# A fixed TensorE order for a two-layer hybrid trunk, and the first norm weight applied at the split

## The chip, the cores and the metric

One core of a Trainium2 chip runs the whole program. The metric is the device time of one execution in microseconds, as the median of several runs. The engines are TensorE (PE, with its weight loads as PEld), VectorE (DVE), ScalarE (ACT), GpSimd (POOL) and SyncE (SP); SP issues the DMAs in the kernel before, one after the other, and a DMA whose buffer isn't free yet holds up those behind it.

## The reference

Two layers over 256 tokens of width 1024, in float32. Each layer is a token mixer and a channel mixer, each between two RMS norms:

```python
def rms_norm(x, g):
    y = xf * lax.rsqrt(jnp.mean(xf * xf, axis=-1, keepdims=True) + NORM_EPS)
    return (y * g.astype(jnp.float32)).astype(x.dtype)

for l in range(DEPTH):
    h = rms_norm(x, ln_mix_pre[l])
    x = x + rms_norm(hybrid_mixer(h, ...), ln_mix_post[l])
    h = rms_norm(x, ln_ffn_pre[l])
    x = x + rms_norm(conv_ffn(h, ...), ln_ffn_post[l])
```

`hybrid_mixer` projects h by `w_in` (2726 columns) for three groups of heads: six with a T5 relative bias on their logits (with 256 tokens and blocks of 256 they are plain causal attention), four with low-rank latents of q and kv and a rotary part, six with a decay from a cumulative sum of log-sigmoids. Their outputs are joined and multiplied by `w_o`. `conv_ffn` multiplies by `w_up` (5632 columns), runs a causal convolution of width 3 over tokens, forms gelu(g) * val, and multiplies by `w_down`.

## The kernel before

**Tiles.** The tokens are two tiles of 128 rows, `xt[0]` and `xt[1]`. `prenorm(t, g)` squares a tile on ACT (`rstd2`, two halves of 512 columns), makes the factor r on POOL, multiplies by the norm weight and by r on DVE. `to_feat(t, ...)` transposes the result on PE, eight blocks of 128x128 in two banks of four, and `split` makes a rounded part (`xh`, ACT) and the rest (`xl`, DVE) of it. Every product is then made of three: high by high, high by low, low by high (`mm3`, `mm3s`, lines 203 to 213).

**Weights.** They are read in slabs of 256 to 512 KB in a fixed order (`plan`): for each layer `c` (latents), `v`, `qa`, `uq`, `uk`, `f`, `qc`, `o`, and then by pairs of feed-forward columns `g`, `u` and `d`. A slab lands in one of three staging buffers `st` (line 175), and `load_next` splits it into `wh` on ACT (line 193) and `wl` on DVE (line 194), for eight slabs at a time. `slab(key)` asks for five slabs ahead and for two more DMAs.

**The start of layer 0.** SP loads tile 0, the identity, and the norm weight, which `gain` reads as a broadcast to 128 rows; then slabs, tile 1 and small constants. Three matmuls of zeros (line 122) stand at the start of PE. The projection `c` of a tile is four pieces (`nat_piece`, one per slab, six matmuls each of 416 columns), `v` is four of 384. `bias_start` builds the bias table from `oh` and `rel_bias` with a matmul (line 286), writes it out and reads it back shifted as `hk`; `bias_end` takes it up later. `c_norm` and `c_feat` norm and transpose the latents (line 373), `mla_up` and `mla_feat` build the four latent heads, and `qk_group` makes the q and k features that `qk_end` copies out (line 402).

**Attention.** `step(n, per)` makes the logits of pair n of heads (`pair_qk`), fills with pieces of other products from the list `fill` (`pump` takes pieces until their listed cost is used up), transposes the softmax of pair n-1 (`pair_t`, copy `pS` at line 512) and forms its output (`pair_pv`, `mh` and `ml`). `wo_piece(t, k)` is one slab of the output projection. Only here was the order of PE the program's:

```python
        with tc.manual_schedule(engines={mybir.EngineType.PE}):
            for n in range(5):
                step(n, total / 5)
```

Everywhere else a scheduler orders each engine's instructions from its own cost model and from priorities (`first` raises those of a function). **Feed-forward.** `up_nat` makes the first two pairs in the natural layout, `up_feat` transposes them, `up(i)` makes the others; `conv_glu` follows on ACT and DVE, and `down(i, t)` adds a pair into the two banks `ac[t]`. The last pairs of tile 1 are held back (`late`) so that tile 0 can be normed beside them.

## Time and profile before

| what | value |
|---|---|
| median of 3 runs | 671.79 us (671.17 to 673.45) |
| the profiled execution | 671.39 us |
| its span in the trace | 669.6 us |
| PE busy in the span | 633.5 us, 95% |
| DVE, ACT, POOL busy | 455.6, 387.0, 30.3 us |
| read from memory | 108.37 MB |
| mean granted clock of PE | 0.984 |

The span is the stretch that the trace covers; the execution's own time holds it and 1.8 us around it. A busy PE is one whose matmuls overlap in the pipeline, so its share says where it stood still, not how near it is to its peak.

### The profile page before, as it was taken

To read this page: it belongs to the slowest core of one execution; us is meant where nothing else is said; L and a number is where in the kernel's file an instruction comes from. 1 tells how busy PE (TensorE), PEld (TensorE's weight loads), DVE (VectorE), ACT (ScalarE), POOL (GpSimd) and SP (SyncE) were. 2 spreads that over 40 slices of the span, in tenths; PEclk is the share of its full clock that TensorE was granted. 3 is DMA by queue.
4 is the path that set the end of the run, shared out by engine and by line. 5 is a ranking of instruction groups with operands and counts; after the bars stand their busy time and mean duration, and the time that the engine had idled before them with its cause. 6 is when DMAs were issued, how large, how long until landed. Compare 5 with 4: busy or idle time off the path is not lost.

```text
span 669.6 us, 11313 instructions
## 1 busy us (share of the span) xinstructions
PE 633.5 (95%) x4286; PEld 572.5 (85%) x4286; DVE 455.6 (68%) x904; ACT 387.0 (58%) x729; POOL 30.3 (5%) x68
## 2 busy tenths in 40 slices
PE   6399999998999999999999999999899999999996
PEld 4299888767899999999979988876899999999995
DVE  4446577657686777777787758765768687777773
ACT  5246676664675655555475757566476465555541
POOL 1110000011000000000023000001200000000001
PEclk7699999999999999999999999999999999999999
DMA  7747562225556665554457865223455765565411
GB/s 242 241 132 213 161 198 73 64 94 188 163 185 215 212 201 189 187 179 141 148 146 201 223 182 185 73 64 95 154 170 180 230 211 189 188 189 189 156 66 63
DMA packets 79668, 110.16 MB, mean 165 GB/s; under 512 B 3960, under 2 KB 69758, under 8 KB 79614
## 3 DMA queue, kind: packets, MB, share of 16 engines
q1 hardware_dynamic: 79614, 109.44, 52.1%
q8 instruction: 33, 0.54, 0.4%
q14 instruction: 21, 0.17, 0.1%
HBM read 108.37 MB, written 1.06 MB: 163 GB/s over the span
## 4 chain that ended last, share of the span: by engine, by line
PE 75%; DMA 10%; ACT 6%; DVE 4%; issue 2%; POOL 2%; SPq 0%; POOLq 0%; DVEq 0%; ACTq 0%
PE wk L210 15%; PE wk L211 15%; PE wk L213 15%; PE wk L203 7%; PE wk L205 7%; PE wk L204 7%; DMA st<-in_w_in_dram 5%; DMA st<-in_w_up_dram 3%; ACT wh L193 3%; DVE wl L194 3%; ACT scr L232 2%; PE wk L510 1%; PE wk L484 1%; PE wk L519 1%; PE wk L482 1%
## 5 line engine op out<-in xcount | busy, mean ns | idle before, releaser
L194 DVE TENSOR_TENSOR wl<-st,wh 128x1024 fp32r<-128x1024 f32 (+3 forms) x200 | 235.8, 1185 | 111.2 <-ACT wh L193 110.3
L193 ACT ACTIVATE wh<-st 128x1024 fp32r<-128x1024 f32 (+3 forms) x200 | 205.0, 1028 | 109.4 <-PE wk L211 33.6
L210 PE MATMUL wk<-xh,wh 128*128 128x256 f32 x768 | 195.2, 286 | 0.0
L211 PE MATMUL wk<-xl,wh 128*128 128x256 f32 x768 | 192.8, 283 | 0.0
L210 PEld LDWEIGHTS wk<-xh,wh 128*128 128x128 f32 x768 | 146.9, 191 | 2.2 <-issue 0.9
L211 PEld LDWEIGHTS wk<-xl,wh 128*128 128x128 f32 x768 | 147.0, 191 | 1.1 <-issue 0.3
L213 PE MATMUL wk<-xh,wl 128*128 128x256 f32 x768 | 123.7, 283 | 0.0
L213 PEld LDWEIGHTS wk<-xh,wl 128*128 128x128 f32 x768 | 106.0, 192 | 0.3 <-issue 0.3
L203 PE MATMUL wk<-wh,hp 128*128 128x512 f32 x176 | 68.8, 391 | 0.0
L204 PE MATMUL wk<-wl,hp 128*128 128x512 f32 x176 | 68.7, 390 | 0.0
L205 PE MATMUL wk<-wh,hp 128*128 128x512 f32 x176 | 68.6, 390 | 0.0
L210 PE MATMUL wk<-wh,xh 128*128 128x256 f32 (+3 forms) x224 | 67.8, 321 | 0.5 <-ACT xh L216 0.5
L211 PE MATMUL wk<-wl,xh 128*128 128x256 f32 (+3 forms) x224 | 66.8, 317 | 1.5 <-DVE wl L194 1.4
L730 ACT ACTIVATE t<-wk,cv 128x256 f32<-128x256 f32 x88 | 44.3, 557 | 33.0 <-PE wk L213 30.8
L734 DVE SCALAR_TENSOR_TENSOR t<-wk,cv,t 128x255 f32<-128x255 f32 x88 | 41.6, 477 | 31.3 <-ACT t L730 31.3
L213 PE MATMUL wk<-wh,xl 128*128 128x256 f32 (+3 forms) x224 | 47.6, 316 | 0.0
L210 PEld LDWEIGHTS wk<-wh,xh 128*128 128x128 f32 x224 | 43.6, 195 | 3.0 <-issue 1.5
L211 PEld LDWEIGHTS wk<-wl,xh 128*128 128x128 f32 x224 | 43.7, 195 | 2.5 <-DVE wl L194 2.2
L736 DVE SCALAR_TENSOR_TENSOR t<-wk,cv,t 128x254 f32<-128x254 f32 x88 | 41.7, 478 | 1.3
L205 PEld LDWEIGHTS wk<-wh,hp 128*128 128x128 f32 x176 | 33.0, 188 | 7.1 <-DVE hp L217 0.2
L203 PEld LDWEIGHTS wk<-wh,hp 128*128 128x128 f32 x176 | 33.1, 188 | 6.7 <-ACT hp L216 0.4
L204 PEld LDWEIGHTS wk<-wl,hp 128*128 128x128 f32 x176 | 33.1, 188 | 6.1
(136 smaller groups left out, 694.9 us busy)
## 6 DMA issues: line engine op xcount, KB each, us to landing
st<-in_w_up_dram SPq DMA_DIRECT2D x88, 512.0 KB, 4.2
st<-in_w_down_dram SPq DMA_DIRECT2D x44, 512.0 KB, 4.3
st<-in_w_in_dram SPq DMA_DIRECT2D x24, 512.0 KB, 4.7
st<-in_w_o_dram SPq DMA_DIRECT2D x16, 512.0 KB, 4.3
st<-in_w_in_dram SPq DMA_DIRECT2D x8, 416.0 KB, 3.7
st<-in_w_in_dram SPq DMA_DIRECT2D x8, 390.0 KB, 4.8
st<-in_w_in_dram SPq DMA_DIRECT2D x8, 384.0 KB, 3.4
x<-in_x_dram SPq DMA_DIRECT2D x2, 512.0 KB, 3.4
```

The lines of the kernel that those rows point to most:

```text
L193: nc.scalar.activation(h[:, c], st[:, c], AF.Copy)
L194: nc.vector.tensor_tensor(lo[:, c], st[:, c], h[:, c].bitcast(F32), op=ALU.subtract)
L203: nc.tensor.matmul(o, stat[0], mov[0], start=start, stop=False)
L204: nc.tensor.matmul(o, stat[0], mov[1], start=False, stop=False)
L205: nc.tensor.matmul(o, stat[1], mov[0], start=False, stop=stop)
L210: nc.tensor.matmul(o, stat[0], mov[0], start=start and i == 0, stop=False)
L211: nc.tensor.matmul(o, stat[0], mov[1], start=False, stop=False)
L213: nc.tensor.matmul(o, stat[1], mov[0], start=False, stop=stop and i == n - 1)
L232: nc.scalar.activation(junk[:, HALF[i]], src[i], AF.Square, scale=1.0 / 32, accum_out=ms[:, i:i + 1])
L730: nc.scalar.activation(y[:, g, :], u[:, g, :], AF.Identity, scale=cv[:, 88 + cj:89 + cj], bias=cv[:, 132 + cj:133 + cj])
L734: nc.vector.scalar_tensor_tensor(y[:, g, 1:], u[:, g, :S - 1], cv[:, 44 + cj:45 + cj], y[:, g, 1:], op0=ALU.mult, op1=ALU.add)
L736: nc.vector.scalar_tensor_tensor(y[:, g, 2:], u[:, g, :S - 2], cv[:, cj:cj + 1], y[:, g, 2:], op0=ALU.mult, op1=ALU.add)
```

## The change

The order of PE's instructions is the program's order from the start to the end, no longer only in attention. So the order in the text is written out anew in several places:

- Layer 0's norm weight isn't broadcast: `g8` holds it as 8x128, one small transpose makes `gT` (128x8), and `to_feat` applies it per block of 128 in the split (`scale=` on ACT, a scalar operand on DVE). `prenorm` with `g=None` only scales by r.
- Tile 0 is loaded in two halves; the identity, `g8`, `oh` and `rel_bias` come over ACT's queue, the bias table goes over POOL's. The constants `cst` come in two parts, and the loads of norm weights stay at their place in SP's order.
- The first pieces `c` go: tile 0's first three, tile 1's transposes, then both tiles' alternately; `v` alternates by slab; then the bias matmul and both tiles' latents. `after` (new) ties the first slab conversions and tile 1's norm behind given instructions.
- The third `qa` group is filler of step 0, the third `qc` group filler of step 5, and the pieces of `wo` move to steps 6 and 7 and to the unrolled end.
- The feed-forward part starts in another order, `down` runs bank by bank over a pair, and the last late pieces run bank by bank.
- There is one more warm matmul.

The diff, without unchanged lines:

```diff
-from contextlib import ExitStack
+from contextlib import ExitStack, contextmanager
...
     def gain(ap):
...
-        nc.sync.dma_start(g, bcast(ap, D))
+        tc.keep_in_program_order(nc.sync.dma_start(g, bcast(ap, D)))
...
-    nc.sync.dma_start(xt[0], x_v[0])
-    nc.sync.dma_start(ident, cst_d[:, 0:128])
-    g_pre = gain(ln_mix_pre[0])
+    ctx.enter_context(tc.manual_schedule(engines={mybir.EngineType.PE}))
+    g8 = work.tile([8, 128], F32, name="g8", tag="pS", bufs=3)
+    oh = work.tile([32, 256 + HA], F32, name="oh", tag="pr", bufs=5)
+    gT = const.tile([128, 8], F32, name="gT")
+    for c in (slice(0, 512), slice(512, 1024)):
+        nc.sync.dma_start(xt[0][:, c], x_v[0][:, c])
+    nc.scalar.dma_start(ident, cst_d[:, 0:128])
+    nc.scalar.dma_start(g8, ln_mix_pre[0].rearrange("(c p) -> c p", p=128))
+    nc.scalar.dma_start(oh[:, :256], oh_d)
+    nc.scalar.dma_start(oh[:, 256:], rel_bias)
+    g_pre = None
...
-    for i in range(3):
+    for i in range(4):
...
     def scr():
...
+    scaled = [None]
...
     def prenorm(t, g):
...
+        src = xt[t] if g is None else hn
+        if g is not None:
+            for c in HALF:
+                nc.vector.tensor_tensor(hn[:, c], xt[t][:, c], g[:, c], op=ALU.mult)
...
-            nc.vector.tensor_tensor(hn[:, c], xt[t][:, c], g[:, c], op=ALU.mult)
-        for c in HALF:
-            nc.vector.tensor_scalar(hn[:, c], hn[:, c], r, None, op0=ALU.mult)
+            scaled[0] = nc.vector.tensor_scalar(hn[:, c], src[:, c], r, None, op0=ALU.mult)
...
+    ends = []
+    @contextmanager
+    def after(*insts):
+        with ExitStack() as st:
+            for i in insts:
+                st.enter_context(tc.issue_after(getattr(i, "ins", i)))
+            yield
...
-    def to_feat(t, hn, xh, xl):
+    def to_feat(t, hn, xh, xl, g=None):
...
-            s = (slice(None), slice(4 * q, 4 * q + 4), tok(t))
-            split(ps, xh[s], xl[s])
+            if g is None:
+                s = (slice(None), slice(4 * q, 4 * q + 4), tok(t))
+                split(ps, xh[s], xl[s])
+                continue
+            for c in range(4):
+                k = 4 * q + c
+                h, gk = xh[:, k, tok(t)], g[:, k:k + 1]
+                a = nc.scalar.activation(h, ps[:, c, :], AF.Copy, scale=gk)
+                v = nc.vector.scalar_tensor_tensor(xl[:, k, tok(t)], ps[:, c, :], gk, h.bitcast(F32),
+                                                   op0=ALU.mult, op1=ALU.subtract)
+            ends.append((a, v))
...
     def postnorm(t, a, g, dst=None):
...
     def bias_start():
-        oh = t2([32, 256 + HA])
-        nc.sync.dma_start(oh[:, :256], oh_d)
-        nc.sync.dma_start(oh[:, 256:], rel_bias)
...
-        rr = t2([HA, 384])
+        rr = work.tile([HA, 384], F32, name="rr", tag="pr", bufs=5)
...
-        nc.sync.dma_start(sd, rr)
+        nc.gpsimd.dma_start(sd, rr)
...
-        nc.sync.dma_start(hk[0], bass.AP(tensor=sd.tensor, offset=sd.offset, ap=[[1, 128], [384, HA], [1, S]]))
+        nc.gpsimd.dma_start(hk[0], bass.AP(tensor=sd.tensor, offset=sd.offset, ap=[[1, 128], [384, HA], [1, S]]))
...
     def bias_end():
...
+        def small_loads():
+            nc.sync.dma_start(lc[:, :256], bcast(q_norm[l], 256))
+            nc.sync.dma_start(lc[:, 256:384], bcast(kv_norm[l], 128))
+            nc.sync.dma_start(lc[:, 384:390], bcast(b_f[l], 6))
         if l == 0:
...
-            hn = [prenorm(0, g_pre), None]
+            hn = [prenorm(0, None), None]
+            dma_next()
+            nc.sync.dma_start(xt[1], x_v[1])
...
-            nc.sync.dma_start(xt[1], x_v[1])
-            to_feat(0, hn[0], xh, xl)
-            slab((l, "c", 0))
-            hn[1] = prenorm(1, g_pre)
+            small_loads()
+            nc.sync.dma_start(cst[:, C_R:], cst_d[:, 128 + C_R:])
+            ps8 = wk()
+            nc.tensor.transpose(ps8[:, :8], g8, ident[:8, :8])
+            nc.vector.tensor_copy(gT, ps8[:, :8])
+            to_feat(0, hn[0], xh, xl, gT)
+            with after(scaled[0]):
+                load_next()
+            for i in range(2):
+                with after(*ends[i]):
+                    load_next()
+            with after(*ends[1]):
+                hn[1] = prenorm(1, None)
         else:
...
             act_set(EXP_SET)
...
-        nc.sync.dma_start(lc[:, :256], bcast(q_norm[l], 256))
-        nc.sync.dma_start(lc[:, 256:384], bcast(kv_norm[l], 128))
-        nc.sync.dma_start(lc[:, 384:390], bcast(b_f[l], 6))
+        cps = [wk(), wk()]
+        vps = [wk(), wk()]
+        def c_piece(t, h):
+            nat_piece(cps[t], "c", t, 416, h)
+        def v_piece(t, h):
+            nat_piece(vps[t], "v", t, 384, h)
+        def v_end(t):
+            nc.scalar.activation(vs[0][:, 384 * t:384 * t + 384], vps[t][:, :384], AF.Copy)
+        if l == 0:
+            c_piece(0, 0)
+            c_piece(0, 1)
+            c_piece(0, 2)
+            to_feat(1, hn[1], xh, xl, gT)
+            for t, h in ((1, 0), (1, 1), (0, 3), (1, 2), (1, 3)):
+                c_piece(t, h)
+            nc.vector.tensor_copy(identr, ident[:6, :6])
+            cn0 = c_norm(0, cps[0])
+            cn1 = c_norm(1, cps[1])
+            for h in range(4):
+                for t in range(2):
+                    v_piece(t, h)
+            v_end(0)
+            v_end(1)
+            nc.sync.dma_start(cst[:, :C_R], cst_d[:, 128:128 + C_R])
+            bias_start()
+            c_feat(0, cn0)
+            c_feat(1, cn1)
+        else:
+            small_loads()
+            for h in range(4):
+                c_piece(0, h)
+            cn0 = c_norm(0, cps[0])
+            for h in range(4):
+                v_piece(0, h)
+            v_end(0)
+            to_feat(1, hn[1], xh, xl)
+            for h in range(4):
+                c_piece(1, h)
+            cn1 = c_norm(1, cps[1])
+            c_feat(0, cn0)
+            for h in range(4):
+                v_piece(1, h)
+            v_end(1)
+            c_feat(1, cn1)
...
-        cps = nat("c", 0, 416)
-        if l == 0:
-            nc.sync.dma_start(cst, cst_d[:, 128:])
-            nc.vector.tensor_copy(identr, ident[:6, :6])
-            bias_start()
-        cn0 = c_norm(0, cps)
-        vps = wk()
-        for h in range(3):
-            nat_piece(vps, "v", 0, 384, h)
-        to_feat(1, hn[1], xh, xl)
-        nat_piece(vps, "v", 0, 384, 3)
-        nc.scalar.activation(vs[0][:, :384], vps[:, :384], AF.Copy)
-        cps = nat("c", 1, 416)
-        cn1 = c_norm(1, cps)
-        c_feat(0, cn0)
-        vps = nat("v", 1, 384)
-        nc.scalar.activation(vs[0][:, 384:768], vps[:, :384], AF.Copy)
-        c_feat(1, cn1)
...
         if l == 0:
...
-        qk_group("qa", 2, 0)
...
-        def qc_fill(i):
+        def q_fill(nm, i, base):
...
             def piece(a, k0):
...
-                proj(st["ps"][:, a, :], "qc", i, a, k0, xh, xl)
+                proj(st["ps"][:, a, :], nm, i, a, k0, xh, xl)
...
-                    qk_end(i, st["ps"], 6)
-            return [(1.3, lambda a=a, k0=k0: piece(a, k0)) for a in range(2) for k0 in (0, 4)]
-        fill += f_fill(0) + f_fill(1) + qc_fill(0) + [(1.2, fox_sum)] + qc_fill(1)
-        q2 = qc_fill(2)
+                    qk_end(i, st["ps"], base)
+            return [(1.44, lambda a=a, k0=k0: piece(a, k0)) for a in range(2) for k0 in (0, 4)]
+        fill += q_fill("qa", 2, 0) + f_fill(0) + f_fill(1) + q_fill("qc", 0, 6) + [(1.0, fox_sum)]
+        q2 = q_fill("qc", 1, 6)
...
-            fill += [(0.4, lambda i=i: fox_bias(i)), q2[i]]
+            fill += [q2[i], (0.5, lambda i=i: fox_bias(i))]
...
-        with tc.manual_schedule(engines={mybir.EngineType.PE}):
-            for n in range(5):
-                step(n, total / 5)
+        for n in range(5):
+            step(n, total / 5)
+        pump(1e9)
+        fill += q_fill("qc", 2, 6)
+        step(5, 5.7)
+        pump(1e9)
+        for n, wo in ((6, ((0, 0), (0, 1), (0, 2), (0, 3))), (7, ((0, 4), (0, 5)))):
+            fill += [(1.4, lambda t=t, k=k: wo_piece(t, k)) for t, k in wo]
+            step(n, 1.4 * len(wo))
...
-            for n, wo in ((5, ((0, 0), (0, 1), (0, 2))), (6, ((0, 3), (0, 4))), (7, ((0, 5), (1, 0))),
-                          (8, ((0, 6), (1, 1)))):
-                fill += [(1.4, lambda t=t, k=k: wo_piece(t, k)) for t, k in wo]
-                step(n, 1.4 * len(wo))
-                pump(1e9)
-            wo_piece(0, 7)
+        wo_piece(1, 0)
+        pS[7] = pair_t(pr[7])
+        wo_piece(0, 6)
+        ot = wk()[:, :256]
+        pair_pv(hd[7], pS[7], ot)
+        first(split)(ot, mh[:, 7, :], ml[:, 7, :])
+        wo_piece(1, 1)
+        wo_piece(0, 7)
...
-        def down(i, t):
-            for a in range(2):
-                j = 2 * i + a
-                wh, wl = slab((l, "d", j))
-                for n in range(2):
-                    c = slice(n * 512, n * 512 + 512)
+        def down(i, t, ns=(0, 1)):
+            for n in ns:
+                c = slice(n * 512, n * 512 + 512)
+                for a in range(2):
+                    j = 2 * i + a
+                    wh, wl = slab((l, "d", j))
...
+        up_nat(0, 1)
+        up_nat(1, 1)
...
-        up_nat(0, 1)
-        up_feat(0, [wk().rearrange("p (a b) -> p a b", a=2) for _ in range(2)])
-        up_nat(1, 1)
-        us1 = acc()
-        up_feat(1, [us1[a].rearrange("p (a b) -> p a b", a=2) for a in range(2)])
-        ac.extend(acc() for _ in range(2))
+        def feat_us():
+            return [wk().rearrange("p (a b) -> p a b", a=2) for _ in range(2)]
+        up_feat(0, feat_us())
...
+            if i == 2:
+                up_feat(1, feat_us())
+                ac.extend(acc() for _ in range(2))
...
-        for j in late:
-            down(j, 1)
+        down(late.pop(0), 1)
+        for n in range(2):
+            for j in late:
+                down(j, 1, (n,))
```

## Rows read from the trace of the kernel before

**Rows 1.** The page, parts 1 and 5 (mean ns of one, idle before).

```profile
PE 633.5 (95%) x4286; PEld 572.5 (85%) x4286; DVE 455.6 (68%) x904; ACT 387.0 (58%) x729; POOL 30.3 (5%) x68
...
L194 DVE TENSOR_TENSOR wl<-st,wh 128x1024 fp32r<-128x1024 f32 (+3 forms) x200 | 235.8, 1185 | 111.2 <-ACT wh L193 110.3
```

**Rows 2.** Windows of 10 us: engines, PEclk, DMA share, GB/s.

```profile
20.00:30.00 10.00, 0.00 (x0) 0.00 (x0) 4.36 (x11) 3.26 (x7) 1.89 (x4) 0.66 0.96 312
...
180.00:190.00 10.00, 8.43 (x72) 8.23 (x71) 8.20 (x16) 6.83 (x13) 0.00 (x0) 1.00 0.48 159
```

**Rows 3.** Waits of PE over the span: total us, times, longest.

```profile
PE wk L286 <- DMA t<-in_rel_bias_dram: 10.4, 1, 10.4
PE wk L262 <- DVE scr L254: 8.6, 7, 3.9
PE wk L708 <- ACT un L702: 1.6, 1, 1.6
...
PE wk L211 <- DVE wl L194: 1.4, 2, 0.7
PE wk L482 <- ACT q L402: 1.3, 1, 1.3
PE wk L203 <- ACT xh L216: 0.9, 2, 0.5
PE wk L205 <- DVE xl L217: 0.9, 2, 0.5
PE wk L519 <- ACT pS L512: 0.9, 2, 0.5
PE wk L203 <- ACT cT L216: 0.9, 1, 0.9
```

**Rows 4.** Timeline of the first 30 us: start, duration, engine, line.

```profile
1.51 5.09 PE L122 MATMUL wk<-t 128*128 128x512 f32 x6 [1.51 <-DVE t L119]
...
5.88 0.56 POOL L235 TENSOR_TENSOR r<-r,mhalf 128x1 f32<-128x1 f32 x1
8.73 1.29 DVE L252 TENSOR_TENSOR scr<-x,gain 128x512 f32<-128x512 f32 x2 [4.26 <-DMA gain<-in_ln_mix_pre_dram]
...
10.47 1.97 PE L262 MATMUL wk<-ident,scr 128*128 128x128 f32 x8 [3.87 <-DVE scr L254]
...
12.48 0.60 ACT L216 ACTIVATE xh<-wk 128x512 fp32r<-128x512 f32 x1 [0.21 <-PE wk L262]
...
15.69 0.88 DVE L254 TENSOR_SCALAR scr<-scr,r 128x512 f32<-128x512 f32 x2 [0.45 <-POOL r L235]
...
27.15 0.28 ACT L363 ACTIVATE t<-wk 128x128 f32<-128x128 f32 x1 [1.86 <-DVE t L365]
...
28.45 0.35 DVE L365 SCALAR_TENSOR_TENSOR t<-wk,r,lc 128x128 f32<-128x128 f32 x1 [1.33 <-POOL r L222]
```

**Rows 5.** Timeline of PE, 31 to 49 us.

```profile
31.26 0.69 PE L210 MATMUL wk<-wh,xh 128*128 128x384 f32 x1
...
36.90 0.34 PE L210 MATMUL wk<-wh,xh 128*128 128x384 f32 x1
...
38.99 0.35 PE L210 MATMUL wk<-wh,xh 128*128 128x416 f32 x1
...
43.14 0.54 PE L213 MATMUL wk<-wh,xl 128*128 128x416 f32 x2
...
48.02 0.49 PE L373 MATMUL wk<-ident,t 128*128 128x128 f32 x3
```

**Rows 6.** Timeline of PE at the boundary of the layers.

```profile
346.06 1.09 PE L262 MATMUL wk<-ident,scr 128*128 128x128 f32 x8 [0.86 <-DVE scr L254]
...
355.52 1.09 PE L262 MATMUL wk<-ident,scr 128*128 128x128 f32 x8 [0.65 <-DVE scr L254]
```

**Rows 7.** DMA issues: count, KB each, median us to landing.

```profile
st<-in_w_in_dram SPq DMA_DIRECT2D x8, 416.0 KB, 3.7
...
hk<-sd SPq DMA_DIRECT2D x1, 768.0 KB, 4.9
```


## The prediction

> **What bounds the kernel now.** I read the page first. TensorE (PE) is busy 633.5 of 669.6 us [rows 1], so about 36 us of the span hold no matmul, and only those, and stretches at the low clock, can be won: the diff removes no matrix work (it adds one warm matmul and one small transpose). Next I read busy time by stretches of 10 us: between 20 and 30 us PE does nothing at all while the DMA engines are 96% busy [rows 2]. Then the waits of PE, longest in total first [rows 3]. Two thirds of the idle time is at the very start: 10.4 us for the load of `rel_bias`, and within the 8.6 us for `scr` one wait of 3.9 us. The rest are a few waits of some 0.5 to 1.6 us at the seams between stages. No line of that view belongs to the long feed-forward loops.
>
> The timeline of the first 30 us says why [rows 4]. The first tile's factor r is ready at 5.88+0.56 = 6.44 us, but VectorE (DVE) multiplies by the norm weight first, and that 512 KB broadcast lands only at 8.73. The transposes start at 10.47, after the three warm matmuls have run out at 1.51+5.09 = 6.60. Tile 1 is scaled at 15.69. What PE does after that is an order of the scheduler's: the bias-table matmul of line 286 stands ahead of the next weights, and its operand is loaded late on SP's queue. PE resumes with real work at 31.26; a 384-column matmul takes 0.69 us there and 0.34 at 36.90 [rows 5]: for 5.6 us the work ran at the low one of the two clock levels, 1.2 instead of 2.4 GHz, and cost about 2.8 us more. From 48.02, the transposes of the second tile's latents, both kernels do the same matrix work. So I cost the change as the time at which the new kernel gets there, and then the seams.
>
> **The start, step by step.**
> 1. Warm matmuls: six halves took 5.09 us [rows 4], 0.85 each. Eight end at 1.51+6.8 = 8.3 at the low clock.
> 2. Weight taken out of `prenorm`: no wait for the broadcast and no multiplication. The scaled tile is ready at 6.44+0.88 = 7.3 (scaling both halves takes 0.88, as for tile 1 in [rows 4]), so PE, not the tile, decides: transposes begin at 8.3 instead of 10.47, and take 1.97 us at the low clock [rows 4] or 1.1 at the high one [rows 6]. By then PE has worked since 1.51 without a break, and the slow stretch of [rows 5] was over 5.6 us after the work began: I take 1.1 and keep 1.97 for the bound.
> 3. Weight put into the split: eight pieces of 128x128 on ScalarE (ACT), then DVE, instead of two of 128x512. The nearest rows are 0.28 on ACT and 0.35 on DVE [rows 4], so 2.2 and 2.8 us against 2x0.60 on ACT: about 1.0 us more on ACT per tile. The first product needs only two pieces, so it starts near 8.9+0.28x2+0.35 = 9.8.
> 4. Until tile 1 is scaled, the old kernel needed 15.69-10.47 = 5.2 us from the first transposes. The new one needs 1.0 more for the pieces, and zero to two slab conversions come ahead of the squares on ACT (the DVE half of one takes 1.19 at 1024 columns [rows 1], some 1.0 at 832). That puts the scaling at 14.5 to 16.3. If the slabs come later, the third piece of tile 0, which stands ahead of tile 1's transposes, waits for its slab instead. I take 16 for the transposes.
> 5. Transposes 1.1 and the first pieces 0.6 to 0.9: 17.8. Left are 5 of the 8 pieces `c`, 30 matmuls. 24 of them take 38.99 to 43.52, 0.19 each [rows 5]: 5.7 us. The 48 of `v` are 384 columns instead of 416: 0.175 each, 8.4 us. Then the bias matmuls (0.5) and the first tile's latents (0.25): 32.6.
>
> So the common point moves from 48.0 to about 32.5: **15.5 us**. The bounds: if step 4 hid altogether, only the work would be left (transposes 2.2, 48x0.19, 48x0.175, 0.75) and the point would be at 8.3+20.5 = 28.8, 19.2 us earlier. If the clock fell in the wait of step 4, the next 5.6 us would cost 2.8 more, and if the first transposes were slow too and a slab late by one conversion, 2 to 3 us more: 10 us earlier.
>
> Whether the clock holds through such waits of one to three microseconds is open. A wait of 1.6 us at line 708 stood in a stretch with granted clock 1.00 [rows 2, 3], the wait of 10.4 stood before one at 1.2 GHz. The Trainium skill, "TensorE: Matmul & The Clock Gate", section "What's actually happening", says that the array is throttled by default, that activity releases it and idleness brings the throttle back; the trace agrees at both ends and is silent between. By that rule taken strictly, the stretch after step 4 is slow and the gain at the start 12.7 instead of 15.5.
>
> Supply: three staging buffers, a landing of 3.7 us [rows 7], and about 1.0 on each of ACT and DVE give a slab every 5.7/3 = 1.9 us. With both tiles' pieces one slab lasts PE 12x0.19 = 2.3 us (`c`) and 2.1 (`v`). So the supply just holds; in the old kernel one slab served one tile at a time. Moving the small loads off SP frees its queue for slabs: the old queue held the `rel_bias` load behind them. I count no bandwidth for the move, since in [rows 2] the DMA engines, not the queue, were full.
>
> The bias table (`hk`, 4.9 us from issue to landing [rows 7]) now goes over POOL's queue; between its matmul and `bias_end` stand two `qa` groups, `mla_up` and `mla_feat`, more than 15 us of PE work, so it costs nothing unless it takes three times as long. The remaining `cst` load and the first layer's post-norm weight come later on SP and delay slabs that PE needs some microseconds later: inside the bounds.
>
> **The seams.**
> - `mla_up` no longer follows its latents at once: the 0.9 us for `cT` [rows 3] goes. -0.9.
> - End of attention: waits for `pS`, `xh`, `xl` of 0.9 each over both layers [rows 3]. The new order puts a piece of `wo` between every evacuation and its use, except before the pair product of step 6, which still follows `pair_t` by one piece. I keep the `pS` wait: -1.8.
> - Boundary of the layers: PE waited 0.86 and 0.65 for the two normed tiles [rows 6] because the transposes had been put ahead of the last late `down` pieces. In program order these pieces come first, and tile 1 has all of `c` and `v` of tile 0 (8.7 us) as cover. Some 0.2 comes back between transposes and first product: -1.3.
> - `qa` 2 is now in the filler of step 0, and step 1 follows at once with the product that reads it. The old kernel shows this pattern once, 1.3 us for `q` [rows 3]. I expect about 1.0 in both layers instead: +0.7.
> - Start of the feed-forward part: the 1.6 us for `un` [rows 3] goes, since a whole `up` stands between. Against it, `to_feat(1)` no longer fills the wait for late slabs (the 1.4 us for `wl`, of which half is here), and `conv_glu(1)` and `conv_glu(2)` fall together behind `up(2)`, with only the two `down(0)`, 5.5 us, as cover. I take 0, with -2 to +4 as ends.
> - Tail: the last `down` pieces end bank 0 earlier, but the bank that ends last still sets the last square: 0.
>
> Sum of the seams: -3.3. Together 15.5+3.3 = 18.8. The profiled execution took 671.4 us (span 669.6 and 1.8 around it), 0.4 below the median shown, 671.8: 671.4-18.8 = **652.6**, and I say 652.5.
>
> **Rivals.**
> - The start gains less. Clock low after step 4 and a late slab: the point is reached at 37 to 38 instead of 32.5, gain 10 to 11, seams as above: 658 to 660. For it: the whole new start hangs on ACT and DVE, which do more small instructions than before; against it: the 10.4 us go in any case.
> - The start gains more. Conversions and squares interleave so that tile 1 is there when tile 0's three pieces end, and the feed-forward seam gives 2: gain 19+5, about 647. Against it: step 4 is a chain through three engines.
> - Slower. The fixed order makes PE wait inside the feed-forward loops: `down` now runs both halves of a pair for bank 0 before bank 1, so its second slab and the second half of `hp` are needed 0.7 us earlier, nine times per layer. To eat 18.8 us it would have to cost over 1.0 us in each of 18 rounds, more than the 0.7 by which the need moves, so it decides only if DVE is already late in each. [rows 3] show no such wait now, and the old order in these loops is already the program's.
> - No net change: the seams' upper ends all at once and the start at its lower bound, near 669. A sum of mishaps, so little.
>
> **How the numbers follow.** Forecast (648 to 656) 0.62; less at the start 0.19 (656 to 664); more 0.12 (under 648); no net change 0.03; slower 0.04. Leaving out half of the second rival and a part of the first and the last two gives 646 to 660. A difference under 0.3%, 2 us, can't be told from none: faster 0.93, same 0.03, slower 0.04.
>
> **What would show it.** Right: the first transposes of tile 0 near 8.3, a granted clock of 1.00 soon after 8 us, no wait at line 286's successor, tile 1's transposes at 15 to 17, the second tile's latents near 32 to 33, no wait for `un` at the start of the feed-forward part, a wait for `q` at step 1 of both layers. Wrong: a second low-clock stretch after 16 us, PE waiting for `wl` between the pieces of `c` and `v`, waits for `hp` at the first `down(1)`, or a wait for `hk` at `bias_end`.

## The result, and the profile after

The changed kernel is slower: 697.6 us (median of four runs, 694.4 to 698.4) against 672.3 (671.2 to 673.5), a ratio of 1.0367 [1.0328, 1.0407]. The forecast was 652.5, so it misses by 45 us and has the wrong sign. The profiled execution took 696.8 us with a span of 695.0.

First the page of the changed kernel, part 1, then the longest waits of PE (total us, times, longest), to be held against [rows 1, 3]:

```profile
PE 645.1 (93%) x4289; PEld 579.5 (83%) x4289; DVE 455.0 (65%) x913; ACT 388.6 (56%) x741; POOL 36.5 (5%) x70
```

```profile
PE wk L283 <- DVE scr L266: 16.0, 3, 8.0
PE wk L211 <- ACT hp L224: 9.0, 3, 4.1
PE wk L510 <- ACT q L430: 7.7, 6, 3.3
```

The wait for `rel_bias` is gone, as forecast. In its place stand three new ones: for the scaled tile at the start of the feed-forward part (L283, twice 7 to 8 us), for `hp` at the first `down(1)` of each layer (L211), and for `q` at the logits (L510, 4.2 of the 7.7 us at the first logits of the two layers). PE is also busy 11.6 us longer on nearly the same matrix work (645.1 against 633.5 in [rows 1]): more of it ran at the low clock, and each of these waits over 3 us has a slow stretch behind it.

Where the time went, from the start of the same PE instruction in both traces:

| point | before | after | lead of the new kernel |
|---|---|---|---|
| transposes of tile 0 | 10.5 | 7.9 | 2.5 |
| transposes of the second latents | 48.0 | 38.3 | 9.7 |
| first logits, layer 0 | 69.9 | 63.8 | 6.1 |
| end of the last `wo` piece, layer 0 | 151.1 | 148.7 | 2.4 |
| feed-forward part, layer 0, first transposes | 152.2 | 156.0 | -3.8 |
| layer 1, first transposes | 346.1 | 357.2 | -11.2 |
| feed-forward part, layer 1, first transposes | 470.8 | 488.1 | -17.4 |
| span | 669.6 | 695.0 | -25.4 |

So the start won 9.7 of the 15.5 us forecast, and 35 us were lost behind it, at few places.

**The late weight.** The timelines of SP, DVE and PE of the changed kernel around the end of the attention part (start, duration, engine, line):

```profile
111.75 34.98 SPq L183 DMA_DIRECT2D st<-in_w_up_dram  x7
146.78 0.50 SPq L105 DMA_DIRECT2D gain<-in_ln_ffn_pre_dram  x1
...
154.19 1.28 DVE L264 TENSOR_TENSOR scr<-x,gain 128x512 f32<-128x512 f32 x2
155.40 0.88 DVE L266 TENSOR_SCALAR scr<-scr,r 128x512 f32<-128x512 f32 x2
...
156.02 1.94 PE L283 MATMUL wk<-ident,scr 128*128 128x128 f32 x8 [7.29 <-DVE scr L266]
```

The norm weight is issued behind seven slabs of `w_up`, and these slabs go out only as staging buffers come free: 35 us for the seven. The two loads of this weight took 7.4 us from issue to landing (first line below, from the list of DMA issues), so this one lands at 154.2, and DVE multiplies by the weight from 154.19 on. In the kernel before, the same load was issued at 27.33 (second line):

```profile
gain<-in_ln_ffn_pre_dram SPq DMA_DIRECT2D x2, 512.0 KB, 7.4
...
27.33 0.42 SPq L105 DMA_DIRECT2D gain<-in_ln_ffn_pre_dram  x1
```

The wait's releaser reads "scr", a DVE tile; one has to go one step further back, to the queue, to find the cause.

**Two `conv_glu` at once.** PE, ACT and DVE of the changed kernel at the start of the loops of layer 0, and windows of the same stretch (length, busy us of PE, PEld, DVE, ACT, POOL, then PEclk, DMA share, GB/s):

```profile
195.41 1.04 PE L786 MATMUL wk<-ident,un 128*128 128x128 f32 x8
...
202.58 0.50 PE L211 MATMUL wk<-wh,hp 128*128 128x512 f32 x1 [0.68 <-ACT hp L224]
...
207.69 0.79 PE L211 MATMUL wk<-wh,hp 128*128 128x512 f32 x1 [4.14 <-ACT hp L224]
...
202.42 2.00 ACT L201 ACTIVATE wh<-st 128x1024 fp32r<-128x1024 f32 x2
...
207.22 0.42 ACT L224 ACTIVATE hp<-hv 128x256 fp32r<-128x256 f32 x1 [2.19 <-DVE hv L819]
...
198.41 0.48 DVE L812 SCALAR_TENSOR_TENSOR t<-wk,cv,t 128x255 f32<-128x255 f32 x1
...
210.72 0.41 DVE L225 TENSOR_TENSOR hp<-hv,hp 128x256 fp32r<-128x256 f32 x1
```

```profile
202.00:206.00 4.00, 0.96 (x3) 0.48 (x3) 3.91 (x11) 3.03 (x6) 0.00 (x0) 1.00 0.00 0
206.00:208.00 2.00, 0.31 (x1) 0.32 (x2) 2.00 (x3) 0.72 (x2) 0.00 (x0) 0.69 0.05 3
208.00:210.00 2.00, 1.86 (x4) 1.02 (x4) 2.00 (x6) 0.83 (x2) 0.00 (x0) 0.50 0.85 263
```

From 198.41 to 211.13 DVE works through both `conv_glu` interleaved, with slab conversions between: 12.7 us, against the two `down(0)` that PE has meanwhile. PE waits 0.7 and 4.1 us, and for the next 5 to 6 us its matmuls take 0.63 instead of 0.39 us, at a granted clock of 0.50, the lower of the two levels.

**The first logits.** ACT and PE:

```profile
60.20 1.06 ACT L201 ACTIVATE wh<-st 128x1024 fp32r<-128x1024 f32 x1 [2.39 <-DMA st<-in_w_in_dram]
61.16 0.36 ACT L430 ACTIVATE q<-wk 128x256 f32<-128x256 f32 x1
61.42 2.03 ACT L470 ACTIVATE q<-wk 96x512 f32<-96x512 f32 x4
63.33 0.40 ACT L430 ACTIVATE q<-wk 128x256 f32<-128x256 f32 x1
...
63.78 0.80 PE L510 MATMUL wk<-q 64*128 64x128 f32 x4 [3.31 <-ACT q L430]
```

The copies of `q` stand on ACT behind a conversion whose slab had not landed. The Trainium skill, "TensorE: Matmul & The Clock Gate" (section "Architectural detail: the array is 16× 32×32, not 1× 128×128"), says that ScalarE works its queue strictly first in, first out; the trace agrees: the first copy starts as the conversion ends. In the kernel before, `qk_group("qa", 2, 0)` gave PE work here; in the new one it is filler of step 0, behind these logits.

**The start.** Windows of the changed kernel, then PE, then ACT and DVE:

```profile
10.00:12.00 2.00, 1.16 (x5) 0.67 (x4) 1.47 (x6) 1.68 (x6) 0.00 (x0) 1.00 0.97 223
12.00:14.00 2.00, 0.97 (x2) 0.55 (x3) 1.52 (x3) 2.00 (x6) 0.19 (x1) 0.55 1.02 337
...
20.00:22.00 2.00, 1.98 (x7) 1.41 (x6) 0.96 (x3) 1.35 (x5) 0.00 (x0) 0.50 0.96 320
22.00:24.00 2.00, 1.58 (x6) 0.86 (x4) 1.61 (x4) 1.96 (x5) 0.00 (x0) 0.89 0.03 12
```

```profile
1.52 5.59 PE L130 MATMUL wk<-t 128*128 128x512 f32 x8 [1.52 <-DVE t L127]
...
7.93 1.09 PE L283 MATMUL wk<-ident,scr 128*128 128x128 f32 x8 [0.67 <-DVE scr L266]
...
12.68 0.72 PE L218 MATMUL wk<-wh,xh 128*128 128x416 f32 x1 [1.32 <-ACT wh L201]
...
16.97 0.71 PE L219 MATMUL wk<-wl,xh 128*128 128x416 f32 x1 [0.78 <-DVE wl L202]
...
18.87 1.91 PE L283 MATMUL wk<-ident,scr 128*128 128x128 f32 x8
...
14.00 0.89 ACT L201 ACTIVATE wh<-st 128x832 fp32r<-128x832 f32 x1
...
15.10 0.88 DVE L266 TENSOR_SCALAR scr<-x,r 128x512 f32<-128x512 f32 x2 [1.16 <-POOL r L243]
15.90 1.95 DVE L202 TENSOR_TENSOR wl<-st,wh 128x832 fp32r<-128x832 f32 x2
```

The transposes of tile 1 have no wait of their own: they stand behind the third piece of `c`, whose slab is ready in both parts only at 16.97. The slab itself is not late: ACT rounds it at 14.00. Its low part `wl` stands on DVE behind the scaling of tile 1, which waited 1.16 us for the factor r. The clock is at its lower level from about 12.2 to 22.4.

### The profile page after: what moved, and what is told of

Same layout as the page of the kernel before. It is cut to its first block, busy times and chain, and to the rows that moved or that the text cites. A ratio compares the mean times of both kernels' runs of the same rounds, so it can differ in the third digit from the quotient of the medians.

```text
span 695.0 us, 11368 instructions
## 1 busy us (share of the span) xinstructions
PE 645.1 (93%) x4289; PEld 579.5 (83%) x4289; DVE 455.0 (65%) x913; ACT 388.6 (56%) x741; POOL 36.5 (5%) x70
## 4 chain that ended last, share of the span: by engine, by line
PE 68%; DMA 10%; DVE 9%; ACT 7%; issue 3%; POOL 1%; SPq 0%; DVEq 0%; POOLq 0%; ACTq 0%
PE wk L218 15%; PE wk L219 14%; PE wk L221 14%; PE wk L211 6%; PE wk L213 6%; PE wk L212 6%; DMA st<-in_w_in_dram 5%; DMA st<-in_w_up_dram 5%; ACT wh L201 4%; DVE wl L202 4%; PE wk L538 1%; PE wk L512 1%; PE wk L510 1%; PE wk L547 1%; DVE t L812 1%
## 5 line engine op out<-in xcount | busy, mean ns | idle before, releaser
L211 PE MATMUL wk<-wh,hp 128*128 128x512 f32 x176 | 71.3, 405 | 9.0 <-ACT hp L224 9.0
L218 PE MATMUL wk<-wh,xh 128*128 128x256 f32 (+3 forms) x224 | 69.9, 329 | 3.6 <-ACT wh L201 1.3
L213 PE MATMUL wk<-wh,hp 128*128 128x512 f32 x176 | 70.5, 400 | 0.3
L212 PE MATMUL wk<-wl,hp 128*128 128x512 f32 x176 | 70.4, 400 | 0.0
L211 PEld LDWEIGHTS wk<-wh,hp 128*128 128x128 f32 x176 | 34.3, 195 | 17.4 <-ACT hp L224 10.9
L241 POOL TENSOR_TENSOR r<-ms,epsb 128x1 f32<-128x1 f32 x16 | 11.1, 695 | 607.5 <-ACT scr L240 607.4
L213 PEld LDWEIGHTS wk<-wh,hp 128*128 128x128 f32 x176 | 34.0, 193 | 9.4 <-DVE hp L225 2.2
```

What stands on the lines that cost most here:

```text
L211: nc.tensor.matmul(o, stat[0], mov[0], start=start, stop=False)
L212: nc.tensor.matmul(o, stat[0], mov[1], start=False, stop=False)
L213: nc.tensor.matmul(o, stat[1], mov[0], start=False, stop=stop)
L218: nc.tensor.matmul(o, stat[0], mov[0], start=start and i == 0, stop=False)
L241: nc.gpsimd.tensor_tensor(r[:, 0:1], ms[:, 0:1], epsb, op=ALU.add)
```

## The experiments

The theory: not the fixing of the order costs, but three places of the new order, which the scheduler had not been bound to before: the late weight, `up_feat(1)` behind `up(2)`, and `qa` 2 behind the first logits; and, smaller, the third piece of `c`. The rival: a fixed order loses time everywhere, whatever it is. All times against the kernel before, 671 to 672 us in each set of runs.

| kernel | median us (range) | ratio to before |
|---|---|---|
| e1_gain_early | 687.9 (687.1 to 689.1) | 1.0241 [1.0219, 1.0262] |
| e2_upfeat_early | 681.9 (680.5 to 684.7) | 1.0155 [1.0123, 1.0186] |
| e4_qa2_back | 690.2 (688.0 to 690.9) | 1.0262 [1.0234, 1.0291] |
| e5_free_order | 660.2 (655.7 to 662.0) | 0.9817 [0.9776, 0.9857] |
| e6_three | 664.8 (664.7 to 665.5) | 0.9905 [0.9885, 0.9925] |
| e7_three_c02 | 662.1 (660.1 to 663.6) | 0.9860 [0.9834, 0.9886] |
| e8_three_start_free | 660.7 (658.8 to 664.1) | 0.9847 [0.9817, 0.9876] |
| e9_free_qa2 | 657.3 (652.9 to 661.6) | 0.9783 [0.9747, 0.9820] |
| e10_no_pin | 687.3 (686.3 to 689.1) | 1.0237 [1.0208, 1.0266] |
| e11_fixed_from_qa | 654.1 (653.7 to 655.1) | 0.9741 [0.9715, 0.9766] |
| e12_feat_under_wo | 659.2 (657.0 to 662.7) | 0.9816 [0.9787, 0.9845] |
| e13_before_fixed | 676.8 (676.4 to 678.0) | 1.0080 [1.0053, 1.0108] |

**e1: the weight issued ahead of the attention steps.**

```
+        g_fpre = gain(ln_ffn_pre[l])
         for n in range(5):
             step(n, total / 5)
...
-        g_fpre = gain(ln_ffn_pre[l])
         postnorm(0, wacc[0], g_post)
```

> The changed kernel with one line moved: the feed-forward norm weight of each layer is asked for ahead of the attention steps instead of just ahead of postnorm. Theory: in the changed kernel the waits of 7.3 and 8.0 us ahead of the transposes at the start of the feed-forward part are the landing of that weight, whose DMA is pinned on SP behind seven slab loads. Then both waits shrink to the 1.1 us of the kernel before, the low clock behind them goes, and the time falls by 14 to 16 us, to about 682. Rival: VectorE is late there because of the slab conversions that stand ahead of the multiplication; then the waits stay above 5 us and the time above 692.

Measured: 9.7 us less, not the 14 to 16 of the theory. The waits for `scr` ahead of the feed-forward part are gone altogether, but part of them comes back one step later, and the first logits of layer 1 wait 3.3 instead of 0.9 us. Why is not shown: here the weight is issued 7 us ahead of them (387.64), but in e10 it is issued 40 us ahead and they wait 5.7. The waits of PE in this kernel:

```profile
PE wk L211 <- ACT hp L224: 9.6, 4, 4.1
PE wk L510 <- ACT q L430: 8.9, 6, 3.3
PE wk L221 <- DVE xl L225: 4.3, 6, 1.4
PE wk L218 <- ACT xh L224: 3.9, 6, 1.4
```

**e2: `up_feat(1)` ahead of `up(2)`.**

```
+        up_feat(1, feat_us())
         late = []
         for i in range(2, NI):
             us = up(i)
             if i == 2:
-                up_feat(1, feat_us())
                 ac.extend(acc() for _ in range(2))
```

> The changed kernel with the transposes of the second feed-forward pair put back ahead of the third pair's up product. Theory: the waits for hp of 0.7+4.1 us in layer 0 and 4.1 in layer 1, and the low clock for some 6 us behind each, come from two conv_glu falling together behind that product; they go, at the price of up to 1 us for un in each layer: 11 to 13 us faster, about 685. Rival: ScalarE and VectorE are behind in their whole queue there, so the wait only moves to the first down of the next pair, and the time stays above 692.

Measured: 15.7 us less, more than expected, and the wait for `hp` has left PE's list. The waits alone were 9.0, and 1.0 came back for `un`; most of the rest is the low clock behind them (some 5 us at half pace in layer 0, and a granted clock of 0.77 from 540 to 550 in layer 1).

**e4: `qa` 2 back ahead of the steps.**

```
             bias_end()
+        qk_group("qa", 2, 0)
...
-        fill += q_fill("qa", 2, 0) + f_fill(0) + ...
+        fill += f_fill(0) + ...
```

> The changed kernel with the third q and k group of attention back ahead of the steps, out of the filler of step 0. Theory: the 3.3 us that the first logits wait in layer 0 (and 0.9 in layer 1) is a copy of q on ScalarE queued behind a slab conversion that waits for its DMA; 5.8 us of other matmuls in between cover it, and the low clock behind it goes: 5 to 7 us faster, about 691. Rival: the slabs are late for TensorE as well, so the group in between waits itself and the time moves by less than 2 us.

Measured: 7.4 us less; no wait is left at the first logits of either layer, and of the 7.7 us for `q` 2.4 are left, at later steps.

**e5: the order fixed in the attention steps alone.**

```
-    ctx.enter_context(tc.manual_schedule(engines={mybir.EngineType.PE}))
...
+        ms = ctx.enter_context(ExitStack())
+        ms.enter_context(tc.manual_schedule(engines={mybir.EngineType.PE}))
         for n in range(5):
             step(n, total / 5)
...
+        ms.close()
         g_fpre = gain(ln_ffn_pre[l])
```

> The changed kernel with TensorE's order fixed only in the attention steps, as in the kernel before; all else as changed. Theory (the pinned weight load and the fixed order are two causes): the waits for the weight stay, 6 and 7 us beyond those of before, and the waits for hp and q go, since the scheduler places the transposes and the logits itself: about 680 to 686. Rival (the fixed order is the whole loss): about 665 or less, below the kernel before, since the start's gain stays.

Measured: 37 us less than the changed kernel and 12 less than the kernel before. Everything else of the change stands here. The theory missed, and the number is the rival's: with this order the weight, too, is issued early (at 11.2, see e10). Which part of the order costs, this run does not tell. The transposes of tile 1 come at 16.23 and those of the second latents at about 33.8:

```profile
33.54 0.87 PE L400 MATMUL wk<-ident,t 128*128 128x128 f32 x6
```

**e6: the three places together, the order fixed everywhere** (the edits of e1, e2 and e4).

> The changed kernel with three places of its fixed order undone together: the weight of the feed-forward part's first norm issued before the attention steps, up_feat(1) ahead of up(2), and qk_group qa 2 back ahead of the attention steps. TensorE's order stays fixed in the whole program. Theory (these three places are most of the loss, each on its own): alone they were worth 9.7, 15.7 and 7.4 us, so 697.6 less 32.8 is some 665 us, and no wait above 2 us is left behind the first 40 us. Rival 1 (the fixed order costs in many small places that the scheduler fills): the sum does not add up, 672 to 680, as the weight's load collides with slabs of the attention part and the freed time turns into waits for slabs. Rival 2 (they overlap the other way: the waits also cost clock behind them, which each cure alone only half returns): under 660, the level of the run with the order fixed only in the steps.

Measured: 664.8, and the three taken one by one give the same (697.6 - 9.7 - 15.7 - 7.4 = 664.8). An agreement to 0.1 us is luck: the spans of the profiled executions give 8.6 + 14.0 + 5.9 = 28.5 against 31.9, and e1 and e2 also changed the waits at the first logits. Within some 3 us it settles the main question: the three costs add up, they are 33 of the 45 us by which the forecast failed, and most of what freeing the order gives back, with the order still fixed. What PE then waits for longest:

```profile
PE wk L221 <- DVE xl L225: 4.1, 6, 1.4
PE wk L218 <- ACT xh L224: 3.9, 6, 1.4
PE wk L510 <- ACT q L430: 2.4, 2, 1.2
```

**e10: the pin taken off the weights' loads, nothing else.**

```
-        tc.keep_in_program_order(nc.sync.dma_start(g, bcast(ap, D)))
+        nc.sync.dma_start(g, bcast(ap, D))
```

> The changed kernel with one part undone: the DMAs of the norm weights are no longer kept in the program's order on the queue (SP), everything else as changed, TensorE's order fixed in the whole program. Theory (the wait ahead of the feed-forward part is the pin's alone): the first feed-forward weight is issued early again, the waits for scr of 7.3 and 8.0 us go, and the time comes to the level of the run that moved this load by hand, 687.9, within 3 us. Rival (the fixed order of TensorE shifts SP's order by itself, so the load stays late without a pin): within 2 us of 697.6.

Measured: 687.3, the level of e1. No wait for `scr` is left ahead of the feed-forward part, but the first logits wait 3.3 and 5.7 us. SP issues the weight 136 us earlier:

```profile
10.64 0.47 SPq L105 DMA_DIRECT2D gain<-in_ln_mix_post_dram  x1
11.15 0.43 SPq L105 DMA_DIRECT2D gain<-in_ln_ffn_pre_dram  x1
```

With the pin and a freer order of PE (e5, e11) the weight is issued early too, at 11.2 and 9.8. So the load is late only where both parts of the change meet. Why the pin holds only then was not examined.

**e7: the third piece of `c` behind tile 1's transposes** (on e6).

```
-            c_piece(0, 2)
             to_feat(1, hn[1], xh, xl, gT)
-            for t, h in ((1, 0), (1, 1), (0, 3), (1, 2), (1, 3)):
+            for t, h in ((1, 0), (1, 1), (0, 2), (0, 3), (1, 2), (1, 3)):
```

> The kernel before it (three places undone) with one more change: in the first layer's start the third piece of c for tile 0 stands behind tile 1's transposes instead of ahead of them. Theory (that piece waits for its slab and holds back the transposes of tile 1, 18.9 instead of the forecast 16): tile 1's transposes come at 16 to 17 and the time falls by 2 to 3 us. Rival (the loads are full until about 16 us and the low clock of this stretch sets the pace): the transposes come earlier, but the second tile's latents stay near 38 us, and the time stays within 1 us.

Measured: 2.7 us less, and the transposes at 15.52 instead of 19.62 in e6:

```profile
15.52 1.97 PE L283 MATMUL wk<-ident,scr 128*128 128x128 f32 x8 [0.69 <-DVE scr L266]
```

Four microseconds at this point become 1.3 at the latents (37.45 against 38.72): the granted clock is 0.50 in this run from about 15 to 25 us. So both readings held in part.

**e8: the start left to the scheduler** (on e6; the order fixed from the first layer's steps on).

> Three places undone, and TensorE's order left to the scheduler up to the first layer's attention steps, fixed from there to the end of the program. Theory (the start as written is also part of the loss): the second tile's latents at about 34 us instead of 38, and 4 to 5 us less than with the order fixed everywhere. Rival (the start loses nothing by its order, the 34 us of the run with free order come from the scheduler's moving work of other stages into it): the latents stay at 37 to 38 and the time is within 1 us.

Measured: 4.2 us less by the medians, the latents at 33.67. In the profiled executions the lead shrinks behind that, from 5.0 us at the latents to 3.9 at layer 1 and 0.8 at the end, so of this size only the start's own part is shown.

**e9: e5 with `qa` 2 back ahead of the steps.**

> TensorE's order fixed in the attention steps 0 to 4 alone (660.2 us), and qk_group qa 2 back ahead of these steps, out of their filler, as in the kernel before. Theory (the first logits wait for the last copy of q because no matrix work stands between, 2.35 and 2.04 us in the two layers, and the clock falls behind): 3 to 5 us less, 655 to 657. Rival (the scheduler can put qa 2 anywhere ahead of the steps, and the filler then lacks it later): within 1 us of 660.

Measured: 657.3, with a range that overlaps e5's, so this run alone decides nothing. The trace speaks for the rival: the first logits still wait 3.3 and 1.2 us, because the scheduler put them ahead of `qa` 2.

**e11: the fixed stretch begun at `qk_group("qa", 0, 0)`** (on e9).

```
+        ms = ctx.enter_context(ExitStack())
+        ms.enter_context(tc.manual_schedule(engines={mybir.EngineType.PE}))
         qk_group("qa", 0, 0)
...
-        ms = ctx.enter_context(ExitStack())
-        ms.enter_context(tc.manual_schedule(engines={mybir.EngineType.PE}))
         for n in range(5):
```

> The version with the order fixed in the attention steps alone and qk_group qa 2 back ahead of them (657.3 us), with the fixed stretch begun three stages earlier, at qk_group qa 0, so that the scheduler can no longer put the first logits ahead of qa 2. Theory (the waits of 3.3 and 1.2 us for q at the first logits are left over because the scheduler took qa 2 from there): 2 to 4 us less, 653 to 655, first logits without a wait over 0.5 us. Rival (the fixed order brings back the waits for wh and q in mla_feat, 1.8 and 1.7 us, which the scheduler covered): within 1.5 us of 657.

Measured: 654.1, the fastest of all by the medians, 17 us under the kernel before and inside the forecast's range, though with another order than the one forecast. It is 3.1 less than e9, but inside e9's range. The first logits have no wait; of the waits that the rival named the one for `wh` came back (1.8) and the one for `q` not (0.2):

```profile
PE wk L282 <- DVE scr L265: 5.3, 8, 1.2
PE wk L509 <- ACT q L429: 2.4, 2, 1.2
PE wk L468 <- ACT wh L200: 1.8, 1, 1.8
...
63.87 0.49 PE L509 MATMUL wk<-q 64*128 64x128 f32 x4
```

**e12: the feed-forward part's first transposes ahead of the last piece of `wo`** (on e7).

```
-        for k in range(2, 8):
+        for k in range(2, 7):
             wo_piece(1, k)
+        to_feat(0, hn0, fh, fl)
+        wo_piece(1, 7)
```

> The fixed order with the three places and the third piece of c undone (662.1 us), and in both layers the transposes of the first tile at the start of the feed-forward part put ahead of the last piece of wo for tile 1, as the scheduler had put them in the kernel before. Theory (with the order fixed, the products behind these transposes wait for their split, 1.3 to 1.4 us twice in each layer, and one piece of wo covers most of it): 3 to 5 us less, 657 to 659. Rival (the transposes come before the scaled tile is ready and PE waits for scr instead): within 1 us of 662, or slower.

Measured: 659.2, 2.9 less by the medians, with ranges that touch. The waits of 1.3 to 1.4 us for the split are gone from both layers, and small ones for `scr` (0.4 and 0.7) and for a late `wl` (0.6 and 1.1) come instead. In the kernel before, these transposes stood behind all of `wo` (152.2, after 1.1 us for `scr`), so this is a new place, where the expectation calls it the scheduler's old one. With this one the order is still fixed everywhere, and the level of e5 is reached: 697.6 - 32.8 - 2.7 - 2.9 = 659.2.

**e13: the kernel before with its own order fixed in the whole program.**

```
+    ctx.enter_context(tc.manual_schedule(engines={mybir.EngineType.PE}))
     nc.sync.dma_start(xt[0], x_v[0])
...
-        with tc.manual_schedule(engines={mybir.EngineType.PE}):
             for n in range(5):
```

> The kernel before with one part of the change alone: TensorE's order fixed in the whole program, in that kernel's own order of its lines. Theory (not the fixing costs, but the places of the new order): its own lines have up_feat(1) ahead of up(2) and qa 2 ahead of the steps, and no load is pinned, so only the seams wait that the scheduler had covered (the split behind to_feat, un, q), 1 to 2 us at some four places in each layer: 676 to 684. Rival (fixing is the loss as such): 690 or more, with new waits also inside the attention steps and the feed-forward loops.

Measured: 676.8, 5.6 us slower than before. Fixing as such costs this much where the lines stand in an order that was never meant for it, by small waits at seams:

```profile
PE wk L287 <- DMA t<-in_rel_bias_dram: 11.9, 1, 11.9
PE wk L214 <- DVE xl L218: 4.2, 5, 2.7
...
PE wk L211 <- ACT xh L217: 2.3, 3, 1.5
```

## Why the prediction was wrong

**The start: the right mechanism, too large.** Transposes of tile 0 came at 7.93 (forecast 8.3) in 1.09 us, the first product at 9.04 (9.8). But step 1 was wrong: it took 0.85 us for each of eight warm halves, and they ended at 7.11 instead of 8.3, the last three 0.43 us apart. (The granted clock reads 1.00 over all of them, so it does not show this.) PE then waited 0.67 us for the scaled tile, so the tile decided, where step 2 has PE decide, and that 7.93 lies near 8.3 is in part luck. Step 4 forecast 16 for tile 1's transposes and got 18.87. The text had named the place, the third piece ahead of them, but as a wait for a late slab, and gave it no price; what was late was the slab's low part, behind tile 1's scaling on DVE. Where that piece does not stand ahead the chain gives 15.5 (e7) and 14.8 to 16.2 (e11, e8, e5), as forecast. Step 5 then had the low clock until 22.4 on top. So the gain was 9.7, just under the lower bound of 10, and 14.2 with the order free (48.0 - 33.8), against 15.5. "Silent between", the text said of the clock; now the trace speaks: the lower level came at about 12.2, inside the wait of 1.3 us, with PE busy 1.16 of the 2 us from 10 to 12. The Trainium skill's statement that was weighed there ("TensorE: Matmul & The Clock Gate", section "What's actually happening": idleness brings the throttle back) agrees so far as the clock fell while PE stood still, and the 12.7 that the prediction worked out by it was nearer to the changed kernel's 9.7 than its 15.5.

**The late weight: a step that was left out.** The diff pins the DMA in `gain`; the prediction looked at the pin only for the first layer's post-norm weight and "inside the bounds". It never asked what stands ahead of the pinned `ln_ffn_pre` on SP: the slabs of `wo` and `w_up`, issued as fast as buffers come free. PE waited 7.3 and 8.0 us there; taking the pin off gives back 10.3, since part of the waits comes back behind them. This is the term of the sum that was missing.

**The start of the feed-forward part: sized 0, measured 15.7.** The prediction named the mechanism in so many words, two `conv_glu` behind `up(2)` with 5.5 us of cover, and took 0 with an end of +4. It did not add up what two of them cost DVE. The rows above do: 12.7 us in one go with the conversions, from 198.4 on, where the cover ends at 201.9. PE then waited 4.8 us in layer 0 and 4.1 in layer 1, and the slow stretch behind each cost an estimated 2 to 3 us more (5 to 6 us at half pace in layer 0); moving the line back gave 15.7. A stall that is named needs the same sum as a gain.

**The first logits: not in the sum, measured 7.4.** The forecast's +0.7 was for step 1, and that came: 0.99 us for `q` in both layers. It left out step 0. With `qa` 2 gone from ahead of it, the first logits follow the copies of `q` at once; in layer 0 the copies stand behind a conversion that waits for its slab, so the wait is 3.3 (0.9 in layer 1), and the matmuls behind it run at the lower clock from 64 to 70 us. The old wait of 1.3, taken as the pattern for step 1, was itself one of first logits, in layer 1. Step 1 of the changed kernel, and that wait of the kernel before:

```profile
74.48 0.49 PE L510 MATMUL wk<-q,q 64*128 64x128 f32 x4 [0.99 <-ACT q L430]
...
389.60 0.49 PE L482 MATMUL wk<-q 64*128 64x128 f32 x4 [1.34 <-ACT q L402]
```

**The small seams.** The wait for `cT` went (-0.9), the one for `pS` stayed at 0.9, and those for `xh` and `xl` at `wo` went. At the boundary of the layers the 1.5 us for the tiles became 1.6 for the split behind them (0.39, 0.32, 0.60 and 0.25 in e6), so the forecast -1.3 was not earned. The wait for `un` went from the changed kernel, but came back at 1.0 to 1.5 as soon as `up_feat(1)` stood early again (e2, e6, e7).

**The rivals.** "Slower" had 0.04 and the wrong mechanism: the sign "waits for `hp` at the first `down(1)`" came, but for the two `conv_glu` ahead of it; behind it no wait shows up in the loops. "No net change" was called a sum of mishaps. The mishaps are of different kinds. At `hp` the fixed order took away a cover that the scheduler finds: in e5 `up_feat(1)` still stands behind `up(2)` and DVE works through both `conv_glu` in one go just the same (178.8 to 191.6), but PE first runs the products whose `hp` is ready, then goes on with the next `up`, and 0.4 us of wait is left. At `q` the scheduler finds none (2.35 and 2.04 us at the first logits in e5); there the move of `qa` 2 costs. The weight is late only with the pin and the fixed order together. e6 shows that the costs add; that they were likely together was argued only here, after the fact.

**What stays open.** Of the 45 us, 33 are the three places, 2.7 the third piece and some 3 the transposes under `wo`. The last 7 are probably the low clock in the start and the small waits that these versions keep; they were not separated further. Nor is it shown why the pin holds only with the fixed order, and what sets the wait at the first logits of layer 1 (0.9 to 5.7 us among e1, e2, e10 and the changed kernel).

## What to carry to other kernels

When an order is fixed by hand, go along every line of the new order and ask for each operand when its producer, on its own queue, can be done; a wait that the old trace does not show may be one that the scheduler was covering. Price a named stall like a gain, by adding up the instructions of the engine that is late, and add the slow clock behind it: the cures of `hp` and `q` gave back 15.7 and 7.4 us where the waits that went add up to 9.0 and 5.3, some 2 to 3 us more for each wait of over 3 us. Fix the order only where the trace shows the scheduler's to be worse (e11), and look at each pinned transfer for what stands ahead of it on its queue.

## What the runs showed of the hardware

The clock fell in the start of the changed kernel although PE, once started, was never idle for more than 1.3 us at a time, and it stayed low from 12.2 to 22.4. The length of this slow stretch is not set by the order as written: e7 and e12 have the same order in the start, and there it runs from about 15 to 25 and from 14 to 17 us. From tile 0's transposes to the first tile's latents e7 takes 29.8 us and e12 27.7 (7.66 to 37.45, 8.81 to 36.50), so a sum over the start carries some 2 us that the source does not decide.

Nor does the length of the single wait decide whether the clock falls. In the kernel before, a wait of 1.6 us stood at a granted clock of 1.00 [rows 2, 3], and in e5 one of 2.35 us ahead of the first logits did not lower it, while those of 3.3, 4.1 and 7.3 us in the changed kernel did. But at the same first logits of layer 0 in e1 a wait of 2.10 us had a slow stretch behind it (0.50 from 65 to 68 us).

While DVE worked through both `conv_glu`, the DMA engines moved nothing for 4 us (202 to 206, share 0.00). SP issued the next slab at 206.91, as DVE ended a conversion that began at 205.64 and took 1.21: with the staging buffers full, a late DVE stops the loads too.
